# A ring of eight quarter-sized weight slots, and DRAM weight sums issued during the recurrence

## The chip, the cores and the metric

The kernel runs on one core of one Trainium2 chip. A core has a matrix engine (PE, TensorE), a vector engine (DVE, VectorE), a scalar engine (ACT, ScalarE), a general engine (POOL, GpSimd) and a queue processor (SP, SyncE) that here only issues transfers. Each engine works through its own list of instructions in order, and waits where an operand isn't there yet. Transfers (DMA) are issued by SP, ACT or POOL and carried out by 16 DMA engines that all of them share.

The metric is the device time of one execution in microseconds (us), the median of several runs. Lower is better.

## The reference: what is computed

One layer of a hybrid decoder, 512 positions, model width 1024, float32, batch 1:

```python
h = rmsnorm(x, norm_mix_g)
proj = h @ w_in                       # 1024 -> 9232 columns, split in eleven parts
bg, cg, xv, q, k, v, z, a, b, ga, gb = split(proj)
y_a = (bg * causal_dwconv(cg * xv, conv_a_w)) @ w_a_out
y_b = gdn_branch(q, k, v, z, a, b, ...) @ w_b_out      # gated delta rule, 8 heads of 128
x = x + (sigmoid(ga) * y_a + sigmoid(gb) * y_b) @ w_o
h = rmsnorm(x, norm_ffn_g)
up = causal_dwconv(h @ w_up, ffn_conv_w)               # 1024 -> 2 * 2816
x = x + (silu(gate) * val) @ w_down                    # 2816 -> 1024
return rmsnorm(x, norm_final_g)
```

All of it is float32 in and out. The gated delta rule is a recurrence over the positions, which the kernel handles in blocks of 128 positions for two heads at a time (four pairs of heads).

## The kernel before, in words

**Float32 products.** Every matrix product runs as three products of rounded operands. A weight tile is split into a high part `wh` (rounded by ACT, line 140) and a low part `wl` (the rest, by DVE, line 141); `mm3` then issues high times low, low times high and high times high (all through line 108). So PE can't start on a block of weights before ACT and DVE have split it.

**Jobs.** The whole kernel is one list of jobs, run by `run_jobs` (line 203). A job is a block of weights of 1 MB (four quarters of 128 x 512 float32) and a function that uses it. Jobs 0 to 15 are the k, q, v and z projections of the four pairs of heads, 16 to 19 those of `gb`; while they run, the recurrence of the pairs is woven in (`front`, `mid`, `back`, lines 742 to 1023). Jobs 20 to 31 are the short convolution (`cg`, `xv`, `bg`), 32 to 35 `ga`, 36 to 43 the two output projections `w_a_out` and `w_b_out`, 44 to 50 `w_o`, 51 to 72 the two halves of `w_up` (the FFN stage), and the rest `w_down`.

**Three kinds of block.** A `Block` is four quarters, each split as it is. A `SumBlock` belongs to a product in seven instead of eight partial products (Strassen's scheme in Winograd's form): its quarters are also added and subtracted in place (line 161), and seven tiles are split. A `FormBlock` holds sums of quarters that were formed beforehand in DRAM, for `w_o` and `w_down`.

**Raw slots.** Before the split, a block lies in a raw tile, tag `raw`, of which there are two (`bufs=2`), each of four quarters. `run_jobs` issues the load of block i+2 from SP when job i starts in the program's order: one transfer of 1 MB (line 135). It can go when the last reader of block i's raw tile is done. SP takes its transfers in order, and the small transfers of the recurrence (`gtd`, `Dm`, `ucd`, `UB`, `tbd`, `T`) are in the same queue.

**Sums in DRAM.** `Sums.form` (line 1154) lists the transfers that form those sums, from DRAM to DRAM, 256 KB each, some of them adding to what is there. They are issued by POOL (line 1162): 32 for `w_o` (4 row groups, 8 each), then 80 for `w_down` (10 groups, 8 each). They are metered by `feed` (line 220): POOL copies one element of a raw tile (`gate`, line 222), and so waits until that block has landed, and then issues `FEED = 3` of the transfers. `run_jobs` calls `feed` in job i with the block of job i+2, if that block is marked `fed` (every `Block` and `SumBlock` but those of jobs 51 and 52), and only when the list `adds` isn't empty. `open_conv` fills that list inside job 20, so that the first gate is in job 21.

**The order of the work.** `tick` (line 95) is called after every 2048 columns that PE multiplies and takes a step in each of the lists of waiting work (evacuation of results, splits, the recurrence's steps); fixed numbers of steps (`Y_T`, `Y_M` and so on) hold the recurrence's matmuls back until their inputs should be there. On top of this the compiler's planner orders each engine's instructions by its own estimates of when their inputs will be ready, so an instruction can be put ahead of one that the program has earlier. Where `keep_in_program_order` stands (the gate and the DRAM sums among them) those instructions keep their order among themselves. Once ordered, an engine waits in that order.

Of the kernel before, what the change touches and what calls it, by code (L numbers as in the profile page):

```python
# [9 lines left out]
F32 = mybir.dt.float32  # L10
F32R = mybir.dt.float32r
AF = mybir.ActivationFunctionType
ALU = mybir.AluOpType
# [3 lines left out]
P = 128  # L17
S = 512
# [8 lines left out]
C_BG, C_CG, C_XV, C_Q, C_K, C_V, C_Z, C_GA, C_GB = range(0, 36, 4)  # L27
# [3 lines left out]
WARM = 3  # L31
WQ = 12
FEED = 3
Y_M = 10


# [24 lines left out]
def layer_kernel(ctx, tc, x, norm_mix_g, w_in, w_ab, conv_a_w, gdn_conv_w, gdn_A_log, gdn_dt_bias,  # L61
                 gdn_norm_g, w_a_out, w_b_out, w_o, norm_ffn_g, w_up, ffn_conv_w, w_down,
                 norm_final_g, out):
    nc = tc.nc
    pe, act, dve, pool = nc.tensor, nc.scalar, nc.vector, nc.gpsimd
# [6 lines left out]
    wp = ctx.enter_context(tc.tile_pool(name="wp", bufs=2))  # L72
# [3 lines left out]
    def nm(s):  # L76
        cnt[0] += 1
        return f"{s}{cnt[0]}"
# [5 lines left out]
    chains, mids, backs, evacs, splits, sums_of, adds = (deque() for _ in range(7))  # L84
    nmm = [0]

    def advance(queue, n):
        while n and queue:
            queue[0].step()
            if queue[0].done:  # L90
                queue.popleft()
            else:
                n -= 1
# [9 lines left out]
    def drain(queue):  # L103
        while queue:
            advance(queue, 1)
# [16 lines left out]
            mm(o, ah, bh, False, i == n - 1, free)  # L122


    class Block:
        def __init__(self, src, quarter=(4, P)):
            self.src, self.quarter = src, quarter
            self.raw, self.ready, self.lead, self.fed = None, False, 2, True
            self.wh, self.wl = {}, {}

        def load(self):
            if self.raw is not None:
                return
            self.raw = wp.tile([P, 4, *self.quarter], F32, tag="raw", bufs=2, name=nm("raw"))
            nc.sync.dma_start(out=self.raw, in_=self.src())

        def part(self, name, src):
            wh = self.wh[name] = wp.tile([P, *self.quarter], F32R, tag="wh", bufs=WQ, name=nm("wh"))
# [4 lines left out]
        def split(self):  # L143
            if self.ready:
                return
            self.ready = True
            for q in range(4):
                self.part(q, self.raw[:, q])
                yield


# [1 line left out]
    class SumBlock(Block):  # L153
        def split(self):
            if self.ready:
                return
            self.ready = True
            r = [self.raw[:, q] for q in range(4)]

            def to(q, a, b, op):  # L160
                dve.tensor_tensor(out=r[q], in0=a, in1=b, op=op)  # L161

            self.part("11", r[0])
            yield
            self.part("12", r[1])
            yield
            self.part("22", r[2])
            yield
            to(2, r[3], r[2], ALU.add)
            to(3, r[0], r[3], ALU.subtract)  # L170
            self.part("s3", r[3])
            yield
            to(0, r[2], r[0], ALU.subtract)
            self.part("s2", r[0])
            yield
            to(1, r[1], r[0], ALU.subtract)
            self.part("s4", r[1])
            yield
            self.part("s1", r[2])
            yield  # L180


    class FormBlock(Block):
# [4 lines left out]
        def load(self):  # L188
            if self.raw is not None:
                return  # L190
            self.raw = self.place()
            for lo, hi, src in self.runs:
                nc.sync.dma_start(out=self.raw[:, lo:hi], in_=src)

        def split(self):
            if self.ready:
                return
            self.ready = True
            for q, name in enumerate(self.names):
                self.part(name, self.raw[:, q])  # L200
                yield

    def run_jobs(jobs):
        jobs[1][0].load()
        for i, (block, use) in enumerate(jobs):
            Task(block.split()).finish()
            drain(splits)
            if i + 1 < len(jobs):
                splits.append(Task(jobs[i + 1][0].split()))
            for j, (later, _) in enumerate(jobs[i + 2:i + 5]):  # L210
                if later.lead >= j + 2:
                    later.load()
            if adds and i + 2 < len(jobs) and jobs[i + 2][0].fed:
                feed(jobs[i + 2][0].raw)
            use(block.wh, block.wl)


    gate = const.tile([1, 64], F32, name="gate")

    def feed(raw):  # L220
        el = raw[0:1, 1].rearrange("p k n -> p (k n)") if len(raw.shape) == 4 else raw[0:1, 1]
        tc.keep_in_program_order(pool.tensor_copy(out=gate[:, 0:1], in_=el[:, 0:1]))  # L222
        advance(adds, FEED)


    def piece(w, j, k):
# [157 lines left out]
    def page(tag, name, dtype=F32, up=0):  # L384
        n, more = {"vT": (1024, 64), "Dm": (1024, 64), "kq0": (2048, 64), "KU0": (2048, 64), "AV0": (2048, 64)}.get(tag, (2048, 0))
        return pg.tile([P, n + more], dtype, tag=tag, name=nm(name))[:, up:up + n]

    def by_columns(t, n=S):
        return t.rearrange("p (k n) -> p k n", n=n)
# [23 lines left out]
    tbd = [dram.tile([4, 8, 32, 32], F32, name=f"tbd{p}") for p in range(4)]  # L413

    k_block = Block(lambda: w_in[C_K])
    k_block.raw = wp.tile([P, 4, 4, P], F32, tag="raw", bufs=2, name=nm("raw"))

    def load_k(q):
        nc.sync.dma_start(out=k_block.raw[:, q], in_=w_in[C_K][:, 4 * q:4 * q + 4])

    HS = S // 2

# [54 lines left out]
    with tc.tile_pool(name="st1", bufs=1) as st1:  # L477
# [15 lines left out]
        load_x(0)  # L493
        load_x(1)
        load_k(0)
        wr = st1.tile([P, P], F32, name="wr")
        nc.sync.dma_start(out=wr[0:96], in_=gdn_conv_w.rearrange("o j (c p) -> (o j c) p", p=P))
        nc.sync.dma_start(out=wr[96:120], in_=conv_a_w.rearrange("o j (c p) -> (o j c) p", p=P))
        nc.sync.dma_start(out=wr[120:128], in_=norm_mix_g.rearrange("o (c p) -> (o c) p", p=P))
        ab_raw = st1.tile([P, ND, 16], F32, name="ab_raw")  # L500
        nc.sync.dma_start(out=ab_raw, in_=w_ab)
        load_k(1)
        load_x(2)
        load_x(3)
        load_k(3)
        load_k(2)
        dtb = gs.tile([P, H], F32, name="dtb")
# [54 lines left out]

        def round_k(q):
            wh = k_block.wh[q] = wp.tile([P, 4, P], F32R, tag="wh", bufs=WQ, name=nm("wh"))
            act.copy(out=wh, in_=k_block.raw[:, q])

        def rest_k(q):
            wl = k_block.wl[q] = wp.tile([P, 4, P], F32R, tag="wl", bufs=WQ, name=nm("wl"))
            dve.tensor_tensor(out=wl, in0=k_block.raw[:, q], in1=k_block.wh[q].bitcast(F32), op=ALU.subtract)


        def ab_tile(k):
# [266 lines left out]
    def mid(pr, U, um, T, rest):  # L839
        for _ in range(Y_T if pr else Y_T + Y_M):  # L840
            yield
# [242 lines left out]
    jobs = []  # L1084
# [95 lines left out]
    down_w = Sums("d", w_down, (0, 1, 2, 3, 4, 5, 7, 8, 9, 10))  # L1180
    EIGHT = 6
    o_w = Sums("o", w_o, (0, 1, 2, 3))

    def open_conv():
        drain(evacs)
        drain(chains)
        drain(mids)
        drain(backs)
        p2.close()
        sc = st["sc"] = p3.enter_context(tc.tile_pool(name="sc", bufs=1, side="right"))  # L1190
        st["ya"] = Rows([by_columns(page(n, "ya")) for n in ("kq1", "CT")])
        room["pool"] = sc
        adds.extend((Task(o_w.form()), Task(down_w.form())))

    def open_mix():
        st["mixa"] = Rows([by_columns(page(n, "mixa")) for n in ("KU1", "AV1")])
# [279 lines left out]
        return use  # L1476

    def raw():
        return wp.tile([P, 4, S], F32, tag="raw", bufs=2, name=nm("raw"))

    jobs += [(FormBlock(*o_w.first_pass(p), 2, raw), o_first(p)) for p in range(ND // 2)]
    jobs.append((FormBlock(*o_w.low(), 2, raw), o_low))
# [296 lines left out]
```

## Time and profile before

| | us |
|---|---|
| median of 3 runs | 949.43 |
| the three runs | 951.06, 949.43, 949.36 |
| the profiled execution | 953.14 |
| its span, first to last instruction | 951.3 |
| PE busy (98% of the span) | 936.8 |
| DVE busy (82%) | 779.3 |
| ACT busy (57%) | 545.7 |
| POOL busy (18%) | 171.4 |
| mean granted TensorE clock | 0.994 |

The runs are without the profiler, the profiled execution with it. Of its 953.14 us, 951.3 are the span that all views of the trace cover; the rest lies before the first and after the last instruction. Busy times of different engines overlap.

### The profile page before, as it was taken

The numbers are of one execution on the slowest core, as the hardware profiler recorded it, in microseconds if no ns is written. First come the engines' busy times: TensorE is split into PE (matmuls) and PEld (weight loads), VectorE is DVE, ScalarE is ACT, GpSimd is POOL, SyncE is SP. The second block draws the span as 40 slices with busy tenths as digits, with TensorE's granted clock in tenths as the row PEclk, the third lists the DMA queues.
The fourth block names the chain that finished last, engine by engine and source line by source line (L and its number), as shares of the span: only waits on it lengthen the run. The fifth ranks groups of instructions, "written<-read, shape, count | busy, mean of one in ns | idle before, by whom it ended". The sixth has DMA issues, their size and how long they took to land.

```text
span 951.3 us, 17103 instructions
## 1 busy us (share of the span) xinstructions
PE 936.8 (98%) x6512; PEld 828.4 (87%) x6512; DVE 779.3 (82%) x1448; ACT 545.7 (57%) x1202; POOL 171.4 (18%) x280
## 2 busy tenths in 40 slices
PE   8999999999999999999999999999999999999996
PEld 7888887987889999999888888998899998888885
DVE  5978686898978998999653479999899998969785
ACT  6896756666565645555642245556556556546463
POOL 3330401304110022222332000232222210000000
PEclk9999999999999999999999999999999999999999
DMA  6443412213021477666786545585755774177332
GB/s 230 156 141 98 121 54 90 76 54 98 9 91 46 120 200 160 174 203 165 237 232 151 126 143 191 176 206 189 198 123 206 172 175 136 45 264 234 101 133 89
DMA packets 51890, 138.17 MB, mean 145 GB/s; under 512 B 21691, under 2 KB 22624, under 8 KB 43104
## 3 DMA queue, kind: packets, MB, share of 16 engines
q1 hardware_dynamic: 39120, 107.45, 33.1%
q0 software_dynamic: 12544, 29.37, 16.6%
q8 instruction: 51, 0.84, 0.4%
q14 instruction: 31, 0.25, 0.1%
q10 hardware_dynamic: 144, 0.26, 0.1%
HBM read 133.64 MB, written 32.78 MB: 175 GB/s over the span
## 4 chain that ended last, share of the span: by engine, by line
PE 83%; DVE 7%; ACT 4%; DMA 3%; issue 2%; SPq 0%; POOL 0%; POOLq 0%; DVEq 0%; ACTq 0%
PE ps L108 75%; DVE wl L141 2%; DVE raw L161 2%; PE ps L739 1%; DMA raw<-in_w_in_dram 1%; ACT wh L140 1%; PE ps L774 1%; DMA raw<-in_w_a_out_dram 1%; DMA raw<-in_w_up_dram 1%; PE ps L977 1%; PE ps L997 1%; PE ps L986 1%; DVE c L352 1%; PE ps L965 0%; PE ps L964 0%
## 5 line engine op out<-in xcount | busy, mean ns | idle before, releaser
L140 ACT CAST wh<-raw 128x512 fp32r<-128x512 f32 x377 | 221.4, 620 | 182.8 <-PE ps L108 99.9
L141 DVE TENSOR_TENSOR wl<-raw,wh 128x512 fp32r<-128x512 f32 x377 | 251.1, 687 | 42.9 <-ACT wh L140 39.1
L108 PE MATMUL ps<-hT,wh 128*128 128x512 f32 (+1 forms) x1048 | 283.1, 350 | 0.8 <-ACT hT L555 0.5
L108 PEld LDWEIGHTS ps<-hT,wh 128*128 128x128 f32 x1048 | 183.4, 190 | 21.3 <-ACT hT L555 0.7
L108 PE MATMUL ps<-hT,wl 128*128 128x512 f32 (+1 forms) x524 | 172.6, 343 | 0.0
L108 PE MATMUL ps<-h,wh 128*128 128x256 f32 (+1 forms) x688 | 168.6, 333 | 0.0
L108 PEld LDWEIGHTS ps<-h,wh 128*128 128x128 f32 x688 | 118.5, 189 | 12.7 <-DVE h L1436 0.2
L108 PE MATMUL ps<-h,wl 128*128 128x256 f32 (+1 forms) x344 | 108.1, 332 | 0.0
L108 PEld LDWEIGHTS ps<-hT,wl 128*128 128x128 f32 x524 | 99.5, 190 | 9.7
L108 PE MATMUL ps<-ts,wh 128*128 128x256 f32 x544 | 102.5, 282 | 2.1 <-ACT v L326 1.9
L108 PE MATMUL ps<-wh,xs 128*128 128x512 f32 (+1 forms) x320 | 96.7, 384 | 0.0
L108 PEld LDWEIGHTS ps<-ts,wh 128*128 128x128 f32 x544 | 86.3, 191 | 2.7 <-ACT v L326 2.1
L161 DVE TENSOR_TENSOR raw<-raw 128x512 f32<-128x512 f32 x108 | 74.3, 688 | 1.8
L222 POOL COPY gate<-raw 1x1 f32<-1x1 f32 x38 | 21.4, 564 | 276.1 <-DMA raw<-in_w_up_dram 117.2
L108 PEld LDWEIGHTS ps<-h,wl 128*128 128x128 f32 x344 | 65.2, 189 | 6.3
L108 PEld LDWEIGHTS ps<-wh,xs 128*128 128x128 f32 x320 | 59.7, 188 | 11.9
L108 PE MATMUL ps<-ts,wl 128*128 128x256 f32 x272 | 66.7, 281 | 0.0
L108 PE MATMUL ps<-wl,xs 128*128 128x512 f32 (+1 forms) x160 | 61.5, 384 | 0.0
L108 PE MATMUL ps<-us,wh 128*128 128x256 f32 x320 | 58.1, 278 | 1.2 <-ACT v L326 1.2
L352 DVE SCALAR_TENSOR_TENSOR ct<-ps,wA,ct 128x511 f32<-128x511 f32 (+2 forms) x72 | 53.3, 742 | 4.0 <-ACT ct L349 3.9
L140 ACT CAST wh<-raws 128x512 fp32r<-128x512 f32 x66 | 38.9, 618 | 27.0 <-PE ps L108 9.4
L141 DVE TENSOR_TENSOR wl<-raws,wh 128x512 fp32r<-128x512 f32 x66 | 42.8, 687 | 13.4 <-ACT wh L140 13.4
(340 smaller groups left out, 1642.2 us busy)
## 6 DMA issues: line engine op xcount, KB each, us to landing
raw<-in_w_in_dram SPq DMA_DIRECT2D x35, 1024.0 KB, 5.3
raw<-in_w_up_dram SPq DMA_DIRECT2D x22, 1024.0 KB, 6.2
dv<-in_w_down_dram POOLq DMA_DIRECT2D x50, 256.0 KB, 6.0
raws<-dv SPq DMA_DIRECT2D x8, 768.0 KB, 6.0
ov<-in_w_o_dram POOLq DMA_DIRECT2D x20, 256.0 KB, 5.9
raws<-in_w_down_dram SPq DMA_DIRECT2D x10, 512.0 KB, 4.5
raw<-in_w_a_out_dram SPq DMA_DIRECT2D x4, 1024.0 KB
raw<-in_w_b_out_dram SPq DMA_DIRECT2D x4, 1024.0 KB, 5.8
```

The source lines that it names most:

```text
L108: pe.matmul(o, lhsT=a, rhs=b, start=start, stop=stop, skip_group_check=free)
L140: act.copy(out=wh, in_=src)
L141: dve.tensor_tensor(out=wl, in0=src, in1=wh.bitcast(F32), op=ALU.subtract)
L161: dve.tensor_tensor(out=r[q], in0=a, in1=b, op=op)
L222: tc.keep_in_program_order(pool.tensor_copy(out=gate[:, 0:1], in_=el[:, 0:1]))
L352: dve.scalar_tensor_tensor(out=dst[:, sh:], in0=src[:, :S - sh], scalar=wcol(j), in1=dst[:, sh:], op0=ALU.mult, op1=ALU.add)
L739: pe.transpose(out=o[:, n * P:(n + 1) * P], in_=src[:, n * P:(n + 1) * P], identity=ident)
L774: pe.matmul(o[:, i], lhsT=kqs[:, a, h, 0, sl], rhs=kqs[:, b, h, :, sl], start=a > 0, stop=a + b == 0)
L977: pe.matmul(o[:, 0:P], lhsT=TTf[:, f, :], rhs=rs[h], start=True, stop=True)
L986: pe.matmul(o2[:, 0:P], lhsT=kn[:, f, :], rhs=vns[h], start=True, stop=True)
L997: pe.matmul(o[:, 0:P], lhsT=A[:, f, :], rhs=vns[h], start=True, stop=True)
```

## The change

Three edits go together.

1. The raw tiles become a ring of eight slots of one quarter each, in place of two slots of four quarters. A block holds a list of four such tiles. Its load is four transfers of 256 KB, each into its own quarter and each held back only by that quarter's earlier readers. This holds for `Block`, `SumBlock`, the first block (`k_block`, whose load was in four transfers already) and the `FormBlock`s that lie in the raw ring. The room is the same.
2. The list `adds` is filled before the jobs start, not inside job 20.
3. In jobs 4 to 19 `feed` is called with the next job's block, and issues two transfers; from job 20 on it works as before, with three. In both cases the gate now reads one element of the block's second quarter, and so waits for that quarter's transfer only.

```diff
+CONV = 20
...
+    def raw_tile(*quarter):
+        return wp.tile([P, *quarter], F32, tag="raw", bufs=8, name=nm("raw"))
...
         def load(self):
             if self.raw is not None:
                 return
-            self.raw = wp.tile([P, 4, *self.quarter], F32, tag="raw", bufs=2, name=nm("raw"))
-            nc.sync.dma_start(out=self.raw, in_=self.src())
+            self.raw = [raw_tile(*self.quarter) for _ in range(4)]
+            for q, t in enumerate(self.raw):
+                nc.sync.dma_start(out=t, in_=self.src()[:, 4 * q:4 * q + 4])
...
             for lo, hi, src in self.runs:
-                nc.sync.dma_start(out=self.raw[:, lo:hi], in_=src)
+                if isinstance(self.raw, list):
+                    for q in range(lo, hi):
+                        nc.sync.dma_start(out=self.raw[q], in_=src[:, q - lo])
+                else:
+                    nc.sync.dma_start(out=self.raw[:, lo:hi], in_=src)
...
-            if adds and i + 2 < len(jobs) and jobs[i + 2][0].fed:
-                feed(jobs[i + 2][0].raw)
+            if 4 <= i < CONV:
+                feed(jobs[i + 1][0].raw, 2)
+            elif adds and i + 2 < len(jobs) and jobs[i + 2][0].fed:
+                feed(jobs[i + 2][0].raw, FEED)
...
-    def feed(raw):
-        el = raw[0:1, 1].rearrange("p k n -> p (k n)") if len(raw.shape) == 4 else raw[0:1, 1]
+    def feed(raw, n):
+        el = raw[1][0:1]
+        el = el.rearrange("p k n -> p (k n)") if len(el.shape) == 3 else el
         tc.keep_in_program_order(pool.tensor_copy(out=gate[:, 0:1], in_=el[:, 0:1]))
-        advance(adds, FEED)
+        advance(adds, n)
...
     o_w = Sums("o", w_o, (0, 1, 2, 3))
+    adds.extend((Task(o_w.form()), Task(down_w.form())))
...
         room["pool"] = sc
-        adds.extend((Task(o_w.form()), Task(down_w.form())))
...
     def raw():
-        return wp.tile([P, 4, S], F32, tag="raw", bufs=2, name=nm("raw"))
+        return [raw_tile(S) for _ in range(4)]
```

More of the change, by code (lines that the diff above doesn't have):

```diff
@@ L147, in split @@
             for q in range(4):
-                self.part(q, self.raw[:, q])
+                self.part(q, self.raw[q])
                 yield
@@ L157, in split @@
             self.ready = True
-            r = [self.raw[:, q] for q in range(4)]
+            r = self.raw
             def to(q, a, b, op):
@@ L199, in split @@
             for q, name in enumerate(self.names):
-                self.part(name, self.raw[:, q])
+                self.part(name, self.raw[q] if isinstance(self.raw, list) else self.raw[:, q])
                 yield
@@ L415, in layer_kernel @@
     k_block = Block(lambda: w_in[C_K])
-    k_block.raw = wp.tile([P, 4, 4, P], F32, tag="raw", bufs=2, name=nm("raw"))
+    k_block.raw = [raw_tile(4, P) for _ in range(4)]
     def load_k(q):
-        nc.sync.dma_start(out=k_block.raw[:, q], in_=w_in[C_K][:, 4 * q:4 * q + 4])
+        nc.sync.dma_start(out=k_block.raw[q], in_=w_in[C_K][:, 4 * q:4 * q + 4])
     HS = S // 2
@@ L564, in round_k @@
             wh = k_block.wh[q] = wp.tile([P, 4, P], F32R, tag="wh", bufs=WQ, name=nm("wh"))
-            act.copy(out=wh, in_=k_block.raw[:, q])
+            act.copy(out=wh, in_=k_block.raw[q])
         def rest_k(q):
             wl = k_block.wl[q] = wp.tile([P, 4, P], F32R, tag="wl", bufs=WQ, name=nm("wl"))
-            dve.tensor_tensor(out=wl, in0=k_block.raw[:, q], in1=k_block.wh[q].bitcast(F32), op=ALU.subtract)
+            dve.tensor_tensor(out=wl, in0=k_block.raw[q], in1=k_block.wh[q].bitcast(F32), op=ALU.subtract)
         def ab_tile(k):
```

## The prediction

> **What bounds the kernel now.** I read the page's busy times first, then PE's list of waits, then stage windows cut where the job types change.
>
> ```profile
> span 951.3 us, 17103 instructions
> ...
> PE 936.8 (98%) x6512; PEld 828.4 (87%) x6512; DVE 779.3 (82%) x1448; ACT 545.7 (57%) x1202; POOL 171.4 (18%) x280
> ```
>
> PE is idle for 951.3 - 936.8 = 14.5 us in all. The change takes no instruction from PE, so it can only win idle time or time at a low clock. The stage windows (length, busy time of each engine, granted clock, DMA share, GB/s) say where those are: the recurrence, the convolution and `ga` jobs, a short stretch behind them, the FFN stage.
>
> ```profile
> 25.00:314.00 289.00, 288.19 (x2527) 247.10 (x2526) 235.28 (x588) 191.91 (x535) 60.42 (x94) 1.00 0.28 85
> 314.00:453.00 139.00, 138.82 (x1146) 136.68 (x1145) 128.71 (x205) 76.70 (x159) 30.94 (x52) 1.00 0.66 174
> 453.00:467.00 14.00, 12.07 (x86) 11.77 (x85) 6.92 (x12) 9.42 (x21) 3.93 (x8) 0.88 0.88 257
> ...
> 605.00:800.00 195.00, 193.70 (x1337) 179.96 (x1337) 183.74 (x285) 114.19 (x214) 45.20 (x68) 1.00 0.67 176
> ```
>
> Idle in these: 0.81, 0.18, 1.93 and 1.30 us, 4.22 together. Most of the other ten lies in the first 25 us and behind the last matmul, which the edits hardly touch. The waits of PE, longest in total first:
>
> ```profile
> PE ps L108 <- ACT v L326: 3.1, 2, 1.9
> PE ps L524 <- DVE warm L481: 1.5, 1, 1.5
> ...
> PE ps L739 <- DVE AV L1016: 0.5, 1, 0.5
> ```
>
> The first row is the whole case: two waits, 1.9 and 1.2 us, both for a small copy on ACT (line 326). The first, at 460 us, in the order SP, POOL, DVE, ACT, PE, with one window on the clock:
>
> ```profile
> 452.33 0.33 SPq L135 DMA_DIRECT2D raw<-in_w_a_out_dram  x1
> ...
> 450.07 0.61 POOL L222 COPY gate<-raw 1x1 f32<-1x1 f32 x1 [8.59 <-DMA raw<-in_w_in_dram]
> 450.63 1.55 POOL L1162 DMA_DIRECT2D dv<-in_w_down_dram  x3
> ...
> 449.36 0.69 DVE L161 TENSOR_TENSOR raw<-raw 128x512 f32<-128x512 f32 x1
> 449.96 4.14 DVE L141 TENSOR_TENSOR wl<-raw,wh 128x512 fp32r<-128x512 f32 x6
> ...
> 459.90 1.66 ACT L140 CAST wh<-raw 128x512 fp32r<-128x512 f32 x3 [2.54 <-DMA raw<-in_w_a_out_dram]
> 461.46 0.36 ACT L326 COPY v<-ps 128x256 f32<-128x256 f32 x1
> ...
> 461.88 0.55 PE L108 MATMUL ps<-ts,wh 128*128 128x256 f32 x1 [1.93 <-ACT v L326]
> ...
> 462.00:464.00 2.00, 2.00 (x10) 2.00 (x11) 1.07 (x2) 2.00 (x5) 1.65 (x4) 0.50 0.81 227
> ```
>
> The load of the `w_a_out` block goes at 452.33, when DVE has split the whole older block in that slot. Three DRAM sums had gone 1.7 us before it, and it lands at 459.9, after 7.5 us. ACT has three casts of that block ahead of the copy PE needs, and stands idle for 2.54 us. Then the clock is at half: in 453 to 467 it averages 0.88, which costs 14 x 0.12 = 1.68 us. The second wait, at 780:
>
> ```profile
> 772.20 0.33 SPq L135 DMA_DIRECT2D raw<-in_w_up_dram  x1
> ...
> 765.69 2.49 POOL L1162 DMA_DIRECT2D dl<-in_w_down_dram  x3
> ...
> 779.67 1.66 ACT L140 CAST wh<-raw 128x512 fp32r<-128x512 f32 x3 [3.38 <-DMA raw<-in_w_up_dram]
> 781.23 0.36 ACT L326 COPY v<-ps 128x256 f32<-128x256 f32 x1
> ```
>
> It has the same shape, 7.5 us from issue to use, but the clock stays whole.
>
> **The change part by part.** *Quarter slots.* The transfers as the page lists them:
>
> ```profile
> q0 software_dynamic: 12544, 29.37, 16.6%
> ...
> raw<-in_w_in_dram SPq DMA_DIRECT2D x35, 1024.0 KB, 5.3
> raw<-in_w_up_dram SPq DMA_DIRECT2D x22, 1024.0 KB, 6.2
> ...
> raw<-in_w_in_dram SPq DMA_DIRECT2D x4, 256.0 KB, 6.6
> ...
> raws<-df SPq DMA_DIRECT2D x6, 256.0 KB, 3.3
> raw<-in_w_o_dram SPq DMA_DIRECT2D x4, 256.0 KB, 4.4
> ```
>
> A whole block lands in 5.3 to 6.2 us, a 256 KB load in 3.3 to 4.4 in mid-kernel, 6.6 in the crowded start. In the block that held the slot, the quarter that is split first becomes free after the subtraction at 449.36 and the first of the six splits from 449.96 on, so at about 450.7; the others follow by one split each (4.14 / 6 = 0.69), until 452.3. The first quarter thus goes 1.6 us earlier; SP's issue time (0.33 each) is no limit. With 3.3 to 6.6 us to land it is there by 454.0 to 457.3 instead of 459.9. The third quarter decides, since three casts stand ahead of the copy: issued at 452.3, it lands by 455.6 to 458.9. The copy at 461.46 has to move by 1.93 us, so the casts must be through by 459.5: the first two are done before, and the third then needs its 0.55 from 458.9. That just fits even at the late end. I take the whole 1.93 us (bounds 0 and 1.93). Late next is DVE: it is busy for 128.71 of the 139 us before, so I count no gain beyond the wait itself.
>
> The half clock goes with it in the profiled execution. In the runs without profiler it is not sure that it's there: 951.06 - 949.36 = 1.70 us, just the price of the half-clock stretch, so I suppose that one of three had it and the median hadn't. In the median I count 0 (bounds 0 and 1.7).
>
> The Trainium skill, page "TensorE: Matmul & The Clock Gate", section "Part 1: The HAM clock gate (the "warmup" mystery)", has the clock halve after at least one idle window of about 3.4 us. By that rule a wait of 1.93 us wouldn't halve it, and taking the wait away would win no clock even in the profiled execution. The trace disagrees (0.50 right behind 1.93 us of idle), and the row decides.
>
> *Sums begun early.* There are 32 + 80 = 112 transfers. Each takes 16.6% x 951.3 / 112 = 1.41 us of all DMA engines. Now they take 38 gates:
>
> ```profile
> L222 POOL COPY gate<-raw x38: 173/357/3756, 327.1 to 779.8; 1x1 f32<-1x1 f32 x38
> ...
> 656.48 0.17 POOL L222 COPY gate<-raw 1x1 f32<-1x1 f32 x1 [12.79 <-DMA raw<-in_w_up_dram]
> ```
>
> Afterwards 16 gates x 2 = 32 are `w_o`'s, all in jobs 4 to 19. Jobs 20 to 41 have 22 gates x 3 = 66, and 14 are left for 5 gates in the FFN stage. The fifth gate of that stage is now the one at 656.48; so behind about 657 us no sum is in flight, where today they go on to 780. The second wait has lost its cause: 1.20 us (bounds 0 and 1.20). The convolution has as many sums a job as before.
>
> *What the recurrence pays.* 289 us with a DMA share of 0.28 get 32 x 1.41 = 45 us more. POOL gets 16 copies and 32 issues:
>
> ```profile
> L1162 POOL DMA_DIRECT2D dv<-in_w_down_dram x50 | 35.5, 795 | 10.8 <-issue 9.6 <-DMA raw<-in_w_up_dram 1.2
> L222 POOL COPY gate<-raw 1x1 f32<-1x1 f32 x38 | 21.4, 564 | 276.1 <-DMA raw<-in_w_up_dram 117.2 <-DMA raw<-in_w_in_dram 111.7 <-DMA raw<-in_w_b_out_dram 29.9
> ...
> 66.68 0.35 SPq L135 DMA_DIRECT2D raw<-in_w_in_dram  x1
> 67.20 0.85 SPq L790 DMA_DIRECT2D UB<-ucd  x2
> ...
> DVE TB L816 <- DMA UB<-ucd: 1.9, 1, 1.9
> ```
>
> That is 0.56 + 2 x 0.80 = 2.15 us per job on POOL, which is busy for 60.42 of 289 us. The gate reads a block that was loaded a job earlier, so it rarely waits; it is also a reader of the second quarter's slot, but the slot's next load comes a job or more later. On SP a load is now four issues, and a recurrence transfer behind it goes 3 x 0.35 = 1.05 us later; `UB` is one for which DVE already waits 1.9 us. The steps counted off in ticks hide most of that. I take +0.5 us, half of one such delay on the one pair that has no slack (PE's 0.5 us wait for line 1016); bounds -0.81 (all idle there goes) and +5.4 (below). The quarter loads of the `w_o` blocks and the first block cost nothing: PE is busy throughout there, and that cover is only lost if a block comes over 5 us late.
>
> *Sum.* Profiled execution: 953.14 - 1.93 - 1.68 - 1.20 + 0.5 = 948.8. It lies 3.7 above the median. Median: 949.43 - 1.93 - 1.20 + 0.5 = **946.8**.
>
> **Rivals.** *The first wait stays.* The convolution keeps its three sums a job, and the gate, which waits for one quarter only, lets them go while the last two quarters are still coming. For it: DMA share 0.88 around the wait. Against: the sums then also end earlier. Only the second wait goes: 949.43 - 1.20 + 0.5 = 948.7. The Trainium skill, page "DMA: Bandwidth & Descriptors", section "Anatomy of one DMA — SWDGE (gpsimd) path", gives about 2.0 us plus the bytes at 436 GB/s per transfer, and speaks for this rival: as an estimate from it three quarters in flight together would land only 0.6 us before the whole, and 1.3 us of the wait would stay.
>
> *Slower: POOL in front of the recurrence.* A gate with two issues (2.15 us) stands in POOL's order just ahead of an operation PE soon needs: the `RQ` copies (line 881) and the `fac` powers (line 1008), four each.
>
> ```profile
> 105.82 0.63 POOL L881 COPY RQ<-TT 32x128 f32<-32x128 f32 x2 [1.61 <-DVE TT L874]
> ...
> 136.09 1.64 POOL L1008 TENSOR_TENSOR fac<-fac,nhalf 128x8 f32<-128x8 f32 x1 [20.13 <-DVE fac L1007]
> 156.62 0.63 POOL L881 COPY RQ<-TT 32x128 f32<-32x128 f32 x2 [18.89 <-DVE TT L874]
> ...
> 106.78 0.21 PE L900 MATMUL ps<-T,KU 32*32 32x32 f32 x1
> ```
>
> For it: PE uses the first `RQ` 0.33 us after POOL ends it. Against: POOL mostly idles long ahead of these (20.13, 18.89 us), and the gate would go in that idle time. Each hit costs up to 2.15 - 0.33 = 1.8 us; with three the time is 949.43 - 3.13 + 5.4 = 951.7, and three are where it passes into slower.
>
> *Nothing.* Runs without profiler don't have the waits at all, or other casts take their place: 949.43 + 0.5 = 949.9.
>
> **How the numbers follow.** Forecast 946.8 (own range 945.1, if the median had the half clock, to 947.5): 0.52. First wait stays, 948.7: 0.21. Nothing, 949.9: 0.07. POOL, 951.7: 0.20. About 0.2%, 1.9 us, is what a measurement of this kernel can tell from no change: faster is below 947.5, slower above 951.3. So faster 0.52, same 0.28, slower 0.20. The range runs from 944.3 (949.43 - 1.93 - 1.20 - 1.7, less 0.3 of the recurrence's idle) to 951.8, which holds all cases but the far side of the POOL one.
>
> **What would show it.** Right: no wait for line 326 above 0.5 us in PE's list; clock 1.00 in 453 to 467; the last gate near 657; four loads of 256 KB per block, the first issued before the old block's last split. Recurrence: its PE idle grows from 0.81 by 0.5 or so. Wrong: new PE waits for ACT behind casts anywhere from 314 to 560; PE waits for `RQ` or `AV` of over 1 us; DVE waiting for `UB` or `T` by more than 3 us.

## The result and the profile after

| | before | after |
|---|---|---|
| median of the runs, us | 949.39 | 981.18 |
| the runs, us | 949.08 to 951.06 | 979.53 to 982.78 |
| profiled execution, us | 953.14 | 982.78 |
| its span | 951.3 | 981.1 |

The changed kernel is slower: the ratio is 1.0331, with a 95% interval of 1.0306 to 1.0356, so about 31.8 us. The forecast was 946.8.

From the page of the changed kernel, the span, the busy times and one line of the transfers:

```profile
span 981.1 us, 17705 instructions
...
PE 942.7 (96%) x6512; PEld 832.4 (85%) x6512; DVE 779.8 (79%) x1448; ACT 544.1 (55%) x1200; POOL 168.6 (17%) x285
...
raw<-in_w_in_dram SPq DMA_DIRECT2D x144, 256.0 KB, 3.8
```

The work is the same. PE's idle time grew from 14.5 to 981.1 - 942.7 = 38.4 us, and its busy time by 942.7 - 936.8 = 5.9 us, which is work at half the clock. Together that is the 29.8 us that the span grew by. PE's list of waits in the changed kernel (where PE waits, for whom, total, times, longest) says who kept it idle:

```profile
PE ps L998 <- DVE vn L991: 9.1, 1, 9.1
PE ps L727 <- DVE G L717: 5.3, 1, 5.3
PE ps L109 <- DVE KU L772: 4.1, 1, 4.1
PE ps L751 <- DVE KU L772: 3.7, 1, 3.7
PE ps L882 <- ACT Y L875: 3.5, 1, 3.5
```

All five are waits of the recurrence. The two waits for the small copy on ACT (line 326 before, 338 now) aren't in the list. The two matmuls that had them come later now, because the recurrence before them is longer: at 495.29 us (461.88 before) and 811.32 us (781.65 before). Windows of the changed kernel (length, busy time of PE, PEld, DVE, ACT and POOL, granted clock, DMA share, GB/s) show these two places, and the place of the longest new wait:

```profile
495.00:505.00 10.00, 10.00 (x59) 8.82 (x59) 7.55 (x13) 9.15 (x19) 2.08 (x3) 1.00 1.01 238
805.00:815.00 10.00, 10.00 (x85) 9.83 (x84) 9.93 (x17) 4.53 (x10) 0.00 (x0) 1.00 0.37 123
262.00:266.30 4.30, 0.29 (x2) 0.00 (x0) 0.00 (x0) 0.00 (x0) 0.00 (x0) 1.00 0.95 246
266.30:276.50 10.20, 5.15 (x21) 4.77 (x21) 6.97 (x18) 3.09 (x9) 0.00 (x0) 0.52 0.05 15
```

PE is busy throughout at the old places, with the clock whole. So the two terms that the forecast counted as gains did come. The loss is all in the recurrence, and the last two rows show its shape: PE stands still, from 262.29 us for 9.06 us, and the clock is at 0.52 in the 10 us from 266.30, of which PE works 5.15.

The chain of waits in the changed kernel, from 244 to 275 us, tells how the longest wait of 9.1 us came about (start, length, what):

```profile
250.69 0.62 POOL gate L234
251.31 0.57 POOL dv L1174
251.92 0.75 POOL RQ L893
...
258.37 0.49 POOL dv L1174
...
258.91 0.19 POOL gate L234
...
259.11 0.35 SPq L140
...
260.49 7.36 DMA UB<-ucd
```

One gate goes at 250.69, its sums and the recurrence's own copies follow on POOL, and the next gate goes only at 258.91. SP has a raw load waiting for that gate, because the gate is the last reader of the slot. `UB` stands behind that load on SP. It is issued at 260.12 and has landed at 267.85, after a transfer of 7.36 us. In the kernel before, SP's order at this place was this:

```profile
222.42 1.78 SPq L788 DMA_DIRECT2D ucd<-KU  x4
228.75 0.35 SPq L135 DMA_DIRECT2D raw<-in_w_in_dram  x1
229.28 0.83 SPq L790 DMA_DIRECT2D UB<-ucd  x2
```

There `UB` went 6.9 us after `ucd`; now it is 14.4 us (260.12 against 245.70).

A second thing shows in the row that lists the gates by line (count, shortest, median and longest in ns, first and last start):

```profile
L234 POOL COPY gate<-raw x43: 173/177/2443, 24.1 to 641.3; 1x1 f32<-1x1 f32 x43
```

There are 43 gates, and the first goes at 24.1 us. The description of the change above, and the prediction with it, leave out a branch: since `adds` is filled before the jobs start, the `elif` of `run_jobs` is live in jobs 0 to 3 too. Each of them issues three sums, which makes twelve sums in the first 100 us that nobody had counted. At that place the chain of the changed kernel, from 45 to 75 us, has this row:

```profile
52.13 7.20 DMA gtd<-GT
```

`gtd` is a transfer of 16 KB.

### The profile page after: what moved, and what is told of

Same layout as the page of the kernel before. It is cut to its first block, busy times and chain, and to the rows that moved or that the text cites. A ratio compares the mean times of both kernels' runs of the same rounds, so it can differ in the third digit from the quotient of the medians.

```text
span 981.1 us, 17705 instructions
## 1 busy us (share of the span) xinstructions
PE 942.7 (96%) x6512; PEld 832.4 (85%) x6512; DVE 779.8 (79%) x1448; ACT 544.1 (55%) x1200; POOL 168.6 (17%) x285
## 4 chain that ended last, share of the span: by engine, by line
PE 82%; DMA 5%; DVE 4%; issue 3%; ACT 3%; POOL 2%; SPq 0%; POOLq 0%; DVEq 0%; ACTq 0%
PE ps L109 77%; DMA raw<-in_w_in_dram 2%; DVE ct L364 1%; DMA tbd<-TB 1%; DVE wl L146 1%; PE ps L751 1%; DMA UB<-ucd 1%; DMA gtd<-GT 1%; PE ps L786 1%; PE ps L1009 1%; PE ps L989 1%; PE ps L998 0%; POOL um L805 0%; PE ps L977 0%; PE ps L976 0%
## 5 line engine op out<-in xcount | busy, mean ns | idle before, releaser
L145 ACT CAST wh<-raw 128x512 fp32r<-128x512 f32 x377 | 223.7, 620 | 193.6 <-PE ps L109 90.7
L166 DVE TENSOR_TENSOR raw<-raw,raw 128x512 f32<-128x512 f32 x108 | 74.3, 688 | 5.3 <-POOL gate L234 3.5
```

What stands on the lines that cost most here:

```text
L145: act.copy(out=wh, in_=src)
```

## The experiments

Three theories stood against each other. **A**: SP's raw loads wait for POOL's gates, and the recurrence's transfers queue behind those loads. **B**: the early sums themselves take DMA engines or POOL's time that the recurrence needs. **C**: the ring, with four loads where one was, and the other order that the planner makes of it. Ratios are to the kernel before, measured in the same session (949.4 to 950.4 us). Line numbers in the rows are each kernel's own.

| kernel | raw slots | sums of jobs 4 to 19 | sums of jobs 0 to 3 | median, us | ratio (95%) |
|---|---|---|---|---|---|
| after | ring | 32, gates on raw | 12, gates on raw | 981.18 | 1.0331 (1.0306 to 1.0356) |
| e1 | ring | none | none | 954.22 | 1.0048 (1.0035 to 1.0061) |
| e2 | two whole | 32, on raw | 12, on raw | 958.18 | 1.0076 (1.0051 to 1.0102) |
| e4 | ring | gates alone, on raw | none | 954.01 | 1.0046 (1.0031 to 1.0060) |
| e5 | ring | 32, on raw | none | 967.48 | 1.0184 (1.0167 to 1.0201) |
| e6 | ring | 32, on `wh` | none | 954.87 | 1.0047 (1.0032 to 1.0061) |
| e7 | ring | 32, on `wh` | 12, on `wh` | 965.66 | 1.0162 (1.0139 to 1.0186) |
| e8 | two whole, four loads | none | none | 952.07 | 1.0022 (1.0010 to 1.0034) |
| e9 | two whole to job 19, then quarters | none | none | 947.82 | 0.9975 (0.9964 to 0.9986) |
| e10 | ring | 32, on `wh` | 12 copies of 16 KB, on `wh` | 960.14 | 1.0100 (1.0076 to 1.0124) |
| e11 | ring | 32, on `wh` | 12 copies of 256 KB, on `wh` | 962.08 | 1.0117 (1.0087 to 1.0146) |
| e12 | as e9 | 32, on `wh` | none | 948.10 | 0.9982 (0.9967 to 0.9996) |
| e13 | two whole | 32, on raw | none | 947.68 | 0.9978 (0.9960 to 0.9997) |
| e14 | ring | 32, on `wh` | 12, on `hT` | 965.52 | 1.0164 (1.0145 to 1.0182) |
| e15 | ring | 32, on `wh` | 12 copies of 16 KB, on `hT` | 955.96 | 1.0062 (1.0045 to 1.0079) |

**The ring alone.** The changed kernel, with the sums begun where they were before.

```diff
-            if 4 <= i < CONV:
-                feed(jobs[i + 1][0].raw, 2)
-            elif adds and i + 2 < len(jobs) and jobs[i + 2][0].fed:
+            if adds and i + 2 < len(jobs) and jobs[i + 2][0].fed:
...
-    adds.extend((Task(o_w.form()), Task(down_w.form())))
...
+        adds.extend((Task(o_w.form()), Task(down_w.form())))
```

> The changed kernel with its ring of eight quarter tiles, but the DRAM sums begun where the kernel before begins them: filled in at the convolution, three behind each gate, none in the stages before. Theory A (the raw loads wait in SP's order for the POOL gate that reads the second quarter, and the transfers of the recurrence queue behind them): the recurrence has no gate, so the 29.8 us go; the quarter loads may still take away the 1.93 us wait at 460 us: 945 to 949.5 us. Theory B (the early sums themselves, in the DMA engines and in POOL's order): the same, 945 to 949.5. Theory C (the ring: four issues where one was, another order on SP): most of the 31.8 us stay, 965 us or more, with PE waits of several us in the recurrence.

Measured: 954.22, slower than before by 0.5%, a value that none of the three had. Most of the 31.8 us is not the ring's, which speaks against C as the main cause, but the ring has a price of its own. PE's waits show where:

```profile
PE ps L109 <- DVE KU L770: 3.6, 1, 3.6
```

PE is idle from 58.37 to 62.01. DVE has the two halves of `KU` in this order (start, length, engine, line), here and in the kernel before:

```profile
56.47 0.69 DVE L770 TENSOR_TENSOR KU<-ps,kdv 128x512 f32<-128x512 f32 x1 [0.39 <-ACT junk L769]
...
61.28 0.68 DVE L770 TENSOR_TENSOR KU<-ps,kdv 128x512 f32<-128x512 f32 x1
```

```profile
52.93 0.68 DVE L760 TENSOR_TENSOR KU<-ps,kdv 128x512 f32<-128x512 f32 x1
...
54.31 0.69 DVE L760 TENSOR_TENSOR KU<-ps,kdv 128x512 f32<-128x512 f32 x1
```

With the ring, casts and the next job's convolution steps were ordered between the two halves, and 1.4 us between them became 4.8. Of the second wait, at 780 us, only 0.44 us are left although the sums run as late as before.

**Early sums with whole slots.** The ring is undone, the sums stay early, twelve in jobs 0 to 3 among them.

```diff
-            self.raw = [raw_tile(*self.quarter) for _ in range(4)]
-            for q, t in enumerate(self.raw):
-                nc.sync.dma_start(out=t, in_=self.src()[:, 4 * q:4 * q + 4])
+            self.raw = wp.tile([P, 4, *self.quarter], F32, tag="raw", bufs=2, name=nm("raw"))
+            nc.sync.dma_start(out=self.raw, in_=self.src())
```

> Two slots for whole blocks as before, with one load a block, and the sums begun early exactly as in the changed kernel (jobs 0 to 3 feed three from the block two jobs on, jobs 4 to 19 feed two). Theory A: the next load into a slot still has the POOL gate among that slot's readers, so SP waits as much; it is one load that waits and not up to four: 965 to 985 us. Theory B: 44 sums of about 1.41 us of all DMA engines stand in the same places: 970 to 985 us. Theory C: the ring is gone, so 952 us or less.

Measured: 958.18; four of the five runs had 957 to 959 and one 951.42, which stays unexplained. All three expectations missed. The ring alone costs 4.8 us and the early sums alone 8.8, together 13.6; the change costs 31.8. The two make each other worse. PE's waits have one row that matters for the prediction:

```profile
PE ps L109 <- ACT v L329: 3.1, 1, 3.1
```

It is the wait at 460 us, now at 465 and longer. So in this kernel the early sums didn't remove it. The one at 780 us has gone.

**Gates without sums, and sums without jobs 0 to 3.** Both have the ring. In the first the gates of jobs 4 to 19 stay with nothing behind them, and `adds` is filled in job 20 as before; in the second only jobs 0 to 3 don't feed.

```diff
-                feed(jobs[i + 1][0].raw, 2)
+                feed(jobs[i + 1][0].raw, 0)
```

```diff
-            elif adds and i + 2 < len(jobs) and jobs[i + 2][0].fed:
+            elif i >= CONV and adds and i + 2 < len(jobs) and jobs[i + 2][0].fed:
```

> The ring of quarter tiles with the sixteen gates of jobs 4 to 19 in place, but no transfer behind them, and no feeding in jobs 0 to 3; the sums run from job 20 on as before. Theory A: SP's loads still wait for the gates; the stalls in the middle of the recurrence (9.06 us of PE idle at 262 to 271 us with 5.1 us lost to the half clock behind it, 3.53 us at 120 us with 3.4) come back at least in part: 953 to 965 us. Theory B: no transfer, no cost: 945 to 949.5 us. Theory C: as for the ring alone, 965 or more.

> The changed kernel without the twelve sums that jobs 0 to 3 feed; jobs 4 to 19 feed two each as in the changed kernel. Theory A: the first gate of the start goes with the sums, the gates of the recurrence stay: of the 29.8 us, the start's 13.2 us of PE idle (5.33 + 3.75 + 4.14) and about 6.8 us of half clock go, the rest stays: 959 to 965 us. Theory B, in the form that the twelve sums in the crowded start do it: all stalls of the start go and the later ones, which have other causes, shrink: 946 to 955 us. Theory C: 970 or more.

Measured: 954.01, the time of the ring alone, and 967.48, a value in none of the three ranges. 954.01 lies in A's range, but by the ring's own price: a gate by itself costs nothing, though in the first of the two SP's loads do wait for gates, 29.7 us in all. A in its plain form has fallen. With sums behind the gates 13.5 us more are lost, nearly all at one place: PE waits 10.5 us for `vn`. Up to 230 us the two kernels have the same waits of PE, to within 0.2 us. SP's rows then, first of the kernel with bare gates, then of the one with sums:

```profile
229.88 3.09 SPq L800 DMA_DIRECT2D ucd<-KU  x4
235.53 1.30 SPq L140 DMA_DIRECT2D raw<-in_w_in_dram  x3
237.00 0.87 SPq L802 DMA_DIRECT2D UB<-ucd  x2
```

```profile
229.24 2.85 SPq L800 DMA_DIRECT2D ucd<-KU  x4
234.88 9.37 SPq L140 DMA_DIRECT2D raw<-in_w_in_dram  x3
244.43 1.28 SPq L802 DMA_DIRECT2D UB<-ucd  x2
```

The three loads take 1.30 us to go in the one and 9.37 in the other. POOL's rows say why, first of the kernel with bare gates, then of the one with sums:

```profile
234.85 0.88 POOL L234 COPY gate<-raw 1x1 f32<-1x1 f32 x2
```

```profile
234.22 0.64 POOL L234 COPY gate<-raw 1x1 f32<-1x1 f32 x1
234.81 0.62 POOL L1174 DMA_DIRECT2D ov<-in_w_o_dram  x1
235.47 1.10 POOL L893 COPY RQ<-TT 32x128 f32<-32x128 f32 x2
...
242.35 0.83 POOL L1174 DMA_DIRECT2D ov<-in_w_o_dram  x1
243.22 0.18 POOL L234 COPY gate<-raw 1x1 f32<-1x1 f32 x1
```

Without sums two gates go together at 234.85. With them, the second keeps its place behind the first one's sums, and the planner has put the second sum behind seven microseconds of the recurrence's copies. So the gate, and with it the slot, the load and `UB`, come 7.4 us later. `UB` then takes longer too: from its issue to its use on DVE it is 8.6 us with sums (244.43 to 253.00) and 5.5 without (237.00 to 242.55). The cause needs both: the gate as a reader that the ring waits for, and the sums that push the gate down POOL's list.

**Gates that read no raw tile.** The kernel just shown, with its gates of jobs 4 to 19 on the job's own rounded tile.

```diff
-                feed(jobs[i + 1][0].raw, 2)
+                feed([None, next(iter(block.wh.values())).bitcast(F32)], 2)
```

> As the kernel without the sums of jobs 0 to 3 (967.48 us), and the gates of jobs 4 to 19 read one element of the job's own rounded tile wh in place of a raw tile: the same sums behind the same number of gates, but POOL is no reader of the ring, so no raw load waits for POOL. Theory A in its present form (UB is issued at 244.43 and not 237.00 us, because a raw load ahead of it on SP waits for a gate that stands on POOL behind copies and a sum): the stall of 10.5 us at 246 to 256 us and its half clock go: 952 to 957 us, about the ring alone with its 954.2. Theory B (the sums slow the small transfers through the DMA engines; UB took 8.6 us from issue to use and not 5.5): 962 to 968 us.

Measured: 954.87, against 967.48 with gates on raw tiles and 954.22 without early sums. Theory A in its second form holds: the same 32 sums cost 12.6 us if the gates read raw tiles, and 0.7 us, within the intervals, if they don't. `UB` is issued at 234.53 us here, earlier than in either of the two kernels just shown:

```profile
234.53 0.83 SPq L802 DMA_DIRECT2D UB<-ucd  x2
```

**The start.** In e7 all gates read `wh`, those of jobs 0 to 3 too.

```diff
+            elif i < 4:
+                feed([None, next(iter(block.wh.values())).bitcast(F32)], FEED)
```

> As the changed kernel, all 44 early sums in place, but all gates of jobs 0 to 19 read wh tiles and none a raw tile. Theory A: only the wait of SP's loads for POOL counted, at the start too: 953 to 960 us. Theory B: the 12 sums of jobs 0 to 3 lie in the DMA engines and in POOL's order in the first 100 us in any case, and the start's stalls stay: 10 to 15 us over the kernel with gates on wh from job 4 on, so 964 or more.

Measured: 965.66, 10.8 us more than without the twelve sums. So here it's not SP that waits for POOL. Two kernels put copies of 16 KB or 256 KB in place of the twelve sums (extra copies into memory that nothing reads; the sums themselves come later).

```diff
+            elif i < 4:
+                feed([None, next(iter(block.wh.values())).bitcast(F32)], 0)
+                for n in range(3):
+                    to = dram.tile([P, S], F32, name=nm("idle"))
+                    src = o_w.q[(3 * i + n) % 4][:, 1]
+                    tc.keep_in_program_order(pool.dma_start(out=to[0:8], in_=src[0:8]))
```

> The kernel with gates on wh tiles and sums from job 4 on (954.87 us), with the twelve transfers of jobs 0 to 3 put back on POOL behind their gates, but as copies of 8 rows (16 KB) into memory that nothing reads, so POOL has the same instructions and the DMA engines 1/16 of the bytes. It asks how the twelve sums cost 10.8 us at the start (965.66 against 954.87). If it is POOL's time (gate and issues ahead of the beta chain and others): 960 us or more. If it is the bytes in the DMA engines: 954 to 957.

> The same with the full 256 KB a copy; DVE's order of instructions is the same in both, and the same as in the kernel whose gates all read wh and that had 965.66 us. If POOL's time is it: as the small copies. If it is the bytes: 962 to 968 us.

Measured: 960.14, as expected if POOL's time were the cause, and 962.08, with overlapping intervals. That doesn't tell POOL's time from bytes, since the trace of the first has a wait that the edit itself brought in:

```profile
43.84 0.62 ACT L145 CAST wh<-raw 128x512 fp32r<-128x512 f32 x1 [5.34 <-POOL gate L240]
```

ACT waits 5.34 us to overwrite a `wh` tile that a gate, behind a long run of POOL's small operations, has yet to read. It is theory A again in another ring, and e7 and e11 have it too (5.32 and 5.34 us). So two more kernels had the four gates on `hT`, which is never overwritten in that stage, at the same places in POOL's order.

```diff
-                feed([None, next(iter(block.wh.values())).bitcast(F32)], FEED)
+                feed([None, hT[0][:, 0:1].bitcast(F32)], FEED)
```

> As the kernel whose gates all read wh tiles (965.66 us), with all 44 early sums, but the four gates of jobs 0 to 3 read one element of hT, a tile that stays unchanged through the whole stage. They stand at the same places in POOL's order, so the twelve sums go at the same points, but no cast on ACT and no load on SP waits for POOL to have read. If the gate as a late reader is the cause at the start too (an ACT cast waited 5.34 us for a gate on wh): 955 to 958 us. If the sums' bytes or POOL's time are: 962 or more.

> The same gates on hT, with copies of 16 KB behind them in place of the twelve sums: POOL's time alone, with no late reader and 1/16 of the bytes. Against the kernel with nothing there (954.87): up to 1 us more if POOL's time doesn't matter, 4 or more if it does. The kernel with the full sums over this one is the price of the bytes.

Measured: 965.52 with the sums and 955.96 with 16 KB copies, against 954.87 with neither. The bytes cost 9.6 us, POOL's time about 1 (it can't be told from nothing by the intervals). That is B, at the start. The chain of waits from 45 to 75 us, first with the sums, then with the small copies:

```profile
52.26 7.43 DMA gtd<-GT
...
59.75 4.61 DMA Dm<-gtd
```

```profile
48.90 2.21 DMA gtd<-GT
...
51.17 3.67 DMA Dm<-gtd
```

In the first, six sums were issued from 47.90 to 51.64 us. The 16 KB of `gtd` are issued at 52.26 and take 7.43 us, 5.2 more than in the other, and everything in the chain up to `KU` waits for them. They are also issued 3.4 us later than in the other: behind the first three sums (issued from 23.73 us) a raw load stands in the chain with 6.80 us, from 25.58, which the other kernel's chain doesn't have. In the changed kernel `gtd` takes 7.20 us. Why so small a transfer takes so long is in the last section.

**Four loads without the ring, and the ring without the start.** In e8 the kernel before loads each `Block` in four transfers into its whole slot. In e9 one tile of eight quarters is handed out in halves: a block of the first twenty is loaded as a whole, a later `Block` or `SumBlock` quarter by quarter.

```diff
-            nc.sync.dma_start(out=self.raw, in_=self.src())
+            for q in range(4):
+                nc.sync.dma_start(out=self.raw[:, q], in_=self.src()[:, 4 * q:4 * q + 4])
```

```diff
+    ring = wp.tile([P, 8, S], F32, name="ring", bufs=1)
...
+        r = ring[:, 0:4] if slot[0] % 2 else ring[:, 4:8]
...
+            self.raw = raw_slot(*self.quarter)
+            if slot[0] <= CONV:
+                nc.sync.dma_start(out=self.raw, in_=self.src())
+                return
+            for q in range(4):
+                nc.sync.dma_start(out=self.raw[:, q], in_=self.src()[:, 4 * q:4 * q + 4])
```

> The kernel before, its two whole slots and its sums unchanged, but each block is loaded by four transfers of 256 KB instead of one of 1 MB. It asks what of the ring alone (954.22, with PE waiting 3.64 us at 58 to 62 us) lies in the four issues: casts can start as the first quarter lands, and the planner orders them earlier. If the four issues and the new order do it: 952 to 956 us, with a wait in 40 to 70 us. If the earlier freed quarter slots do it: 948 to 951 us, and the waits at 460 and 780 us stay.

> The first twenty blocks as in the kernel before (two whole slots, one load a block, no sums), and from the twenty-first block on quarters that are loaded and freed one by one; the sums as in the kernel before. The order of the recurrence's instructions is that of the kernel before. If the ring's loss is all at the start and its gain at the two waits (460 and 780 us): 949.4 - 1.93 - 1.20 = 946.3 us, so 945.5 to 947.5. If its loss is elsewhere (more issues or packets everywhere): 949 or more.

Measured: 952.07 and 947.82. The four loads alone cost about 2.3 us, half of the ring's 4.8, with no slot freed any earlier. It isn't the wait for `KU`, which e8 doesn't have; two other waits of the recurrence are longer than before (0.9 us for `G`, 0.7 for `vn`). The two waits on ACT shrink here too: near the first place 0.49 us are left, although the loads of that block go at 452.36 to 453.69 us, no earlier than the one load before (452.33), and of the second 0.69. With the recurrence left as it was and quarters from the convolution on, the kernel is faster than before: 0.9975, or 1.3 to 3.4 us. Its span is 946.0 us. The longest of PE's waits that has to do with the change:

```profile
PE ps L109 <- ACT v L339: 0.8, 1, 0.8
```

The wait at 460 us has gone, and of the one at 780 us 0.75 is left. The median lies just above the range that was expected.

**Both halves without the harm.** e12 is e9 with the 32 early sums and gates on `wh`. e13 is the kernel before with the 32 early sums, no ring, and gates on raw tiles.

```diff
+            if 4 <= i < CONV:
+                feed(None, next(iter(block.wh.values())).bitcast(F32)[0:1, 0], 2)
+            elif i >= CONV and adds and i + 2 < len(jobs) and jobs[i + 2][0].fed:
+                feed(jobs[i + 2][0].raw)
```

> The kernel with two slots up to the twentieth block and quarters from there on (947.82 us), with the sums of jobs 4 to 19 of the changed kernel (two a gate), whose gates read wh tiles. The orders of PE, DVE and ACT are the same as without them. It asks what the early sums are worth once no load waits for POOL. If the sums' bytes cost nothing in the recurrence: 947 to 948, and the last 0.75 us of wait at 775 us may go. If they delay the small transfers: 949 or more.

> Two whole slots as before, sums from job 4 on, two a gate, and the gates read raw tiles as in the changed kernel: the kernel with early sums and two slots (958.18) less the twelve sums of jobs 0 to 3. If the start's twelve sums were most of its 8.8 us: 950 to 953. If the gates on the raw tiles cost as much as with the ring (12.6 us between the gates on raw and on wh): 958 or more.

Measured: 948.10, just above the range expected, and 947.68, below both ranges. Both beat the kernel before, by 0.2%, and neither can be told from e9. The halves of the change win the same two microseconds, not two and two. From e13, PE's remaining wait at 455 us, and SP's wait for gates:

```profile
PE ps L109 <- ACT u L326: 1.0, 1, 1.0
```

```profile
SPq L136 <- POOL gate L225: 43.0, 9, 13.8
```

With two whole slots SP waits for gates for 43.0 us and nothing comes of it: PE has no new wait over 0.5 us in the recurrence. Compared with e2, the twelve sums of jobs 0 to 3 cost 10.5 us here too, without the ring.

## Why the prediction was wrong

The loss adds up along a row of kernels that differ by one step each (medians):

| step | us |
|---|---|
| before, to the ring alone (949.40 to 954.22) | 4.8 |
| 32 sums in jobs 4 to 19 (to 954.87) | 0.7 |
| their gates read raw tiles (to 967.48) | 12.6 |
| 12 sums in jobs 0 to 3 (to 981.18) | 13.7 |

- **The first wait, 1.93 us: right**, and by the cause named. It has gone in e9, where quarters are the only edit. The rival in which it stays fell with that. Most of the gain needs no slot freed earlier, only loads that land by quarters: e8, which frees none earlier, leaves 0.49 us. The prediction's own working has it so, since the third quarter, which decides there, goes no earlier than the old load. Early sums alone left 1.0 us at that block in e13 and made the wait 3.1 us in e2.
- **The second wait, 1.20 us: right in size, half right in cause.** It has gone where the sums end early (e2, e13), as argued, but the quarters alone take most or some of it too (0.44 left in e1, 0.75 in e9). The last gate is at 641.3 us in the changed kernel, which by then runs some 30 us late. The step "the fifth gate of that stage is now the one at 656.48" failed by the twelve sums that weren't counted; in e13, without them, the last gate is at 651.9.
- **"Afterwards 16 gates x 2 = 32 are `w_o`'s, all in jobs 4 to 19": wrong.** Jobs 0 to 3 feed as well. It was a misreading of `run_jobs`, not of the profile, and it cost 13.7 us of the 31.8.
- **"It is also a reader of the second quarter's slot, but the slot's next load comes a job or more later": wrong**, the step that failed for the 12.6 us. The distance was counted in the program's order. The planner had put the gate behind seven microseconds of copies on POOL and the load right ahead of `UB` on SP. The sentence before, that the gate "rarely waits", was true (e4): the harm is not that the gate waits but that it is late and others wait for it.
- **"+0.5 us, bounds -0.81 and +5.4" for the recurrence: too small by a factor of six** even at the upper end. The bound rested on POOL delaying PE through `RQ`, which the changed kernel shows for 1.1 us only. The rival that named POOL had the right engine and the wrong way: POOL delayed SP, and SP delayed `UB`.
- **"The quarter loads of the `w_o` blocks and the first block cost nothing", with no term for those in between beside 1.05 us of issues: wrong** by 4.8 us in all (e1); four loads without a ring cost 2.3 (e8). The prediction took the instructions' order as given. That the new order of `KU` and the casts makes the difference is read from the trace and not tried by itself; what e9 shows is that the loss goes when the recurrence keeps its whole loads.
- **45 us of DMA time in a stage with a share of 0.28, priced at nothing: right for jobs 4 to 19** (0.7 us in e6), wrong for the first 100 us, where 16 KB took 7.43 us (e14).
- **The half clock**: the prediction counted it in the profiled execution alone and 0 in the median. For the kernel before that holds: in the session of e6, 23 of its 28 runs had a mean granted clock of 0.997 or more and none less than 0.996, where the profiled one had 0.994. In the changed kernel half clock added 5.9 us to PE's busy time, behind the new waits. No term had it.
- Signs named as "wrong" came: DVE waited 11.1 us for `UB` and 7.0 for `T`, with 3 as the limit set, and PE 1.1 us for `RQ`, with 1 as the limit.

Open are the one fast run of e2, and how the ring and the twelve sums of the start come to cost 13.7 us together with gates on raw tiles where the bytes alone cost 9.6. The traces show one place: in the chain of the changed kernel a transfer of `tbd` takes 10.51 us from 99.14, and PE then waits 3.5 us for `Y` at 120 us; in e14 `tbd` takes 8.80 us, and PE's wait for `Y` is 0.3. What makes the difference there was not tried by itself.

## What to carry to other kernels

An operation that reads a buffer of a ring only to mark time is still a reader: whoever reloads the buffer waits for it, at the place where it stands in its engine's real order, and everything queued behind that load waits too. Let such a gate read a tile that nobody needs back soon. And before pricing an edit, go through the loop's branches for every value of its index: what is switched on earlier may be live where the text of the change doesn't mention it, and bulk transfers that are free in the middle of a stage aren't where a small transfer on the path has other loads of its own queue ahead of it.

## What the runs showed of the hardware that I had not expected

**A small transfer behind large ones of its own queue.** `gtd` goes from SP's queue (q1), the sums from POOL's (q0). In e14 SP had issued eight raw loads of 256 KB from 37.88 to 49.52 us, before `gtd` at 52.26. The packets of the two queues in e14 from 52.6 to 56.2 us (count, MB, share of the 16 engines):

```profile
q0 software_dynamic: 242, 0.74, 83.9%
q1 hardware_dynamic: 89, 0.16, 12.8%
```

The 0.16 MB of q1 are ten times the size of `gtd`, and none of them are its own: its 32 packets of 512 bytes run from 56.27 to 59.20 us, behind the last packet of the raw loads at 55.04. The sums' packets run beside both, from 49.54 to 59.14. In e15 the raw loads' packets end at 50.08 and those of `gtd` at 50.32. So `gtd` didn't wait until the sums were through. Its packets came behind those of its own queue's loads, which in this stretch got 12.8% of the engines' time beside the 83.9% of the sums. That the sums delay `gtd` mainly through these loads is read from the packets and not tried by itself. The Trainium skill, page "DMA: Bandwidth & Descriptors", section "Queues, rings and completion order", says that a DMA engine takes turns between the queues it has work for, a packet at a time. The trace agrees as far as it shows this: both queues move packets in the stretch above, and again from 56.27 to 59.14 us.

**The half clock comes after less than an idle window.** In each of the traces the changes of the granted clock lie a multiple of 3.41 us apart. Windows of 3.41 us that end where the clock may change, with PE's busy time first and the granted clock third from the end; of the kernel before, of e5 and of e2:

```profile
458.53:461.94 3.41, 1.48 (x14) 1.28 (x12) 1.39 (x3) 2.04 (x5) 1.60 (x4) 1.00 0.82 338
```

```profile
57.70:61.11 3.41, 1.47 (x11) 1.10 (x9) 1.31 (x2) 3.40 (x8) 0.00 (x0) 1.00 0.02 8
61.11:64.53 3.42, 1.27 (x6) 1.05 (x7) 3.41 (x9) 3.23 (x18) 0.40 (x1) 1.00 0.26 81
64.53:67.94 3.41, 3.41 (x10) 2.67 (x9) 3.31 (x14) 1.29 (x7) 1.61 (x1) 0.50 0.26 80
```

```profile
466.97:470.38 3.41, 1.64 (x12) 1.44 (x12) 2.52 (x4) 3.41 (x9) 2.62 (x4) 1.00 0.74 153
470.38:473.79 3.41, 3.41 (x21) 3.08 (x22) 1.59 (x3) 3.41 (x8) 0.63 (x1) 1.00 1.00 170
```

The window of the kernel before, in which PE worked for 1.48 us, was followed by half clock (the prediction shows 0.50 from 462 us). In e5 the one with 1.47 was not, and the next, with 1.27, was. In e2 PE waited 3.07 us at 465.49, longer than the 1.93 of the kernel before, but the wait lay across two windows with 1.93 and 1.64 us of work, and the clock stayed whole. So in these rows the limit lies near 1.5 us of work in a window of 3.41. One window doesn't fit: from 7.97 us in the kernel before PE worked for 1.86 us, and the next was at half. The Trainium skill, page "TensorE: Matmul & The Clock Gate", section "Part 1: The HAM clock gate (the "warmup" mystery)", has the clock go by free-running windows of 3413 ns and halve after at least one idle window. In the steps of 3.41 us the trace agrees; that a whole window has to be idle it doesn't bear out. For a price this means that a wait of 2 to 4 us may cost 1.7 us more (half of 3.41) for each window at half clock behind it, or nothing, depending on where the windows lie.
